# Own places for the first loads, block 0's squares among the sample's tiles, and memory's values for two heads at once

## The chip, the cores and the metric

One core of a Trainium2 chip. The metric is the device time of one execution in microseconds (us), median over runs. The engines work side by side, each on its own instruction queue in order: TensorE (PE; its weight loads are listed as PEld), VectorE (DVE), ScalarE (ACT), GpSimd (POOL), and SyncE (SP), which here only issues DMAs.

## The reference, cut to what matters

A one-layer encoder trunk runs over 1024 prompt tokens and 256 sample tokens, in float32. All projections have 1024 input features.

```python
h = rmsnorm(x, norm_mix_w)
proj = h @ w_in          # DeltaNet q/k/v, decay inputs, gates, spatial-gating halves u and v
...
def spatial_gating_branch(u, v, ln_w, ln_b, w_s, b_s):
    u = jax.nn.gelu(u)
    v = layernorm(jax.nn.gelu(v), ln_w, ln_b)
    ...
def memory_cross_attention(h, mem, w_q, w_kv, w_o):
    q = (h @ w_q).reshape(bsz, seq, XA_HEADS, XA_HEAD_DIM)
    kv = (mem @ w_kv).reshape(bsz, mem.shape[1], 2, XA_HEADS, XA_HEAD_DIM)
    ...
```

The begin of the kernel is the first RMSNorm of the tokens and the product with the columns of w_in for v and the decay inputs (w_sv, 528 columns). "Memory's values" are the second half of kv: 512 normalised memory tokens (256 for each request group) times 1024 x 1024 weights, four heads of 256 columns.

## The kernel before, in words

Activations lie with features on the partitions: eight tiles (k = 0 to 7) of 128 features by n tokens. The tokens form three blocks: block 0 and block 1 (512 prompt tokens each) and block 2, the sample (256 tokens). A product keeps float32 accuracy by three passes: each operand is split into a rounded part hi (ACT copies it to a reduced format) and a rest lo (a subtraction on DVE or POOL), and PE adds hi x hi, lo x hi and hi x lo. `split` (L124 to L126) does that; `split_w` does it for weight tiles, with the rest on POOL until the DeltaNet stage begins, on DVE from there. Weight tiles come in the order of the list `order`; `take` gives the next one and `ahead` splits the one after it. The unsplit weights land in two shared raw buffers.

PE's instructions stay in the order in which the program writes them. The main line of work is written straight on; beside it run side generators, which a planner resumes by its own clock: each matmul adds its columns divided by 2.4 ns, and a side that yields a number of ns is resumed at the first poll (a `yield` of the main line) after that many have passed. So `yield lag` decides how many of the main line's matmuls stand ahead of a side's. Instructions of the other engines are ordered by a list scheduler, by readiness and place in the program.

A norm (class `Norm`) squares each feature tile on ACT (`add`), sums the squares on DVE (L249), lets PE sum over the partitions (a column of ones), takes the inverse root on DVE (L224 to L228, tile nst), lets PE broadcast it, and scales each tile on DVE (`rest`, L284, tile nt). The scaled tile is then split into hi and lo, which are what PE multiplies.

The begin: the sample's x (xs) is loaded, then the first half of w_sv in the two raw buffers, constants, block 0's x (x0) and, when the raw buffers are free again, the second half of w_sv. The sample's norm runs first; block 0's is a side (`other_norms`), whose sum over partitions stands LAG0 = 7500 planner ns behind its begin. `sgv(b)` multiplies a block by both halves of w_sv: for the sample two chunks of 128 tokens by two halves, 24 matmuls of 264 columns each. Then come two gate tiles of the sample (`sgu`), then block 0's `sgv`, which needs block 0's tiles. `ln(cs)` takes the layernorm of v, beginning 1500 planner ns after a block's `sgv`.

Memory's values (`mem_v`): for each head four tiles of 128 memory tokens gather 8 feature tiles in four banks of PSUM, with two weight tiles of 4 features groups x 256 columns; the result is copied by ACT into a staging tile and stored to vd. Meanwhile the sample's DeltaNet scan runs as a side.

Of the kernel before, what the change touches and what calls it, by code (L numbers as in the profile page):

```python
# [17 lines left out]
P = 128  # L18
D = 1024
KT = D // P  # L20
NP, NS = 1024, 256
NTOK = NP + NS
NCH = NTOK // P
NMEM = 256
HEADS = 4
# [16 lines left out]
def f32(ap):  # L42
    return ap.bitcast(F32)
# [11 lines left out]
class Trunk:  # L55
# [44 lines left out]
    def mm(self, out, l, r, start=True, stop=True, more=False):  # L100
        n = 1
        for x in out.shape[1:]:
            n *= x
        if l.dtype == F32R:
            self.clock += max(n, 16) / 2.4 * (1 if n >= 256 else 4)
        else:
            self.clock += (4 * n / 2.4) if n > 1 else 2
        self.nc.tensor.matmul(out, l, r, start=start, stop=stop, skip_group_check=more)  # L108
# [22 lines left out]
    def load(self, i):  # L131
        while self.loaded <= i and self.loaded < len(self.order):
            src = self.order[self.loaded][0]
            raw = self.raw()[:, :1024]
            self.nc.sync.dma_start(raw, src)
            self.raws[self.loaded] = raw
            self.loaded += 1

# [25 lines left out]
def trunk_kernel(ctx: ExitStack, tc: tile.TileContext, a):  # L164
    nc = tc.nc
    V, S, G, T, SY = nc.vector, nc.scalar, nc.gpsimd, nc.tensor, nc.sync
    K = Trunk(ctx, tc, a)
    mm, mm3, tr, split = K.mm, K.mm3, K.tr, K.split
# [7 lines left out]
    wp = K.wp = ctx.enter_context(pool("w", 2))  # L176
    hp = ctx.enter_context(pool("h"))
    pm = ctx.enter_context(pool("pm", 4, space=PSUM))
# [18 lines left out]
        elif job[0] == "gate":  # L197
            order.append((a["w_g"][job[1]], "wp"))
    order += [(a["w_k"][m], "wp") for m in range(KT)]
    order += [(a["w_v"][h, i], "wp") for h in range(HEADS) for i in range(2)]  # L200
    order += [(a["w_ub"][m], "wp") for m in range(KT // 2)]
    order += [(a["w_ua"][m], "wp") for m in range(KT // 2)]
    order += [(a["w_out"][m], "wp" if m < 2 else "wx") for m in range(KT)]
# [13 lines left out]
    def bank(p=pq, tag="b"):  # L217
        return p.tile([P, 512], F32, tag=tag, name="bank")

    def wk(w, k, m=P):  # L220
        return w[0][:, k * m : (k + 1) * m], w[1][:, k * m : (k + 1) * m]
# [66 lines left out]
    def norm(p, xk, n, wcol, sink, pace=1300, step=700, lag=1500):  # L288
        nm = Norm(p, n)
        for k in range(KT):  # L290
            nm.add(xk(k))
            yield step
        yield from nm.rest(xk, wcol, sink, pace, lag=lag)

    def to_h(h, b):
        return lambda k, t: split(h[b][0][:, k, :], h[b][1][:, k, :], t, V if k % 2 else G)
# [37 lines left out]
    def x_load(src, t0, n, name):  # L334
        x = xp.tile([P, KT, 512], F32, tag="x", name=name)[:, :, :n]
        for k in range(0, KT, 2):
            SY.dma_start(x[:, k : k + 2, :], src[:, k : k + 2, t0 : t0 + n])
        return x

    def sv_raw(half):  # L340
        raws = [K.raw() for _ in range(2)]
        for i, raw in enumerate(raws):
            SY.dma_start(raw, a["w_sv"][half][:, i * 1056 : (i + 1) * 1056])
        return raws

    def sv_split(half, raws):
        lo = svp.tile([P, 8 * 264], F32R, tag="lo", name="svl")
        hi = svp.tile([P, 8 * 264], F32R, tag="hi", name="svh")
        for i, raw in enumerate(raws):
            sl = slice(i * 1056, (i + 1) * 1056)  # L350
            split(hi[:, sl], lo[:, sl], raw, V if i else G)
        sv.append((hi, lo))


    xs = hp.tile([P, KT, NS], F32, tag="lo1", name="xs")
    for k in range(0, KT, 2):
        SY.dma_start(xs[:, k : k + 2, :], a["xT"][:, k : k + 2, NP:])
    SY.dma_start(sm, a["small"])
    SY.dma_start(cst[:, C_BD:], a["const"][:, C_BD:])
    sv_raw0 = sv_raw(0)  # L360
    SY.dma_start(cst[:, :C_BD], a["const"][:, :C_BD])
    x_h = act_tiles()

    def first_norm():

        nm = Norm(xp, 512)
        for k in range(0, KT, 2):
            nm.add(xs[:, k : k + 2, :].rearrange("p k t -> p (k t)"))
        nm.n = NS
        yield from nm.rest(lambda k: xs[:, k, :], S_MIX, to_h(x_h, 2), 0, lag=0, halves=2)  # L370

    first = K.side(first_norm())
    sv_split(0, sv_raw0)
    x0 = x_load(a["xT"], 0, 512, "x0")
    sv_split(1, sv_raw(1))
    K.finish(first)

    done = set()

    def other_norms():  # L380
        yield from norm(xp, lambda k: x0[:, k, :], 512, S_MIX, to_h(x_h, 0), 600, 0, LAG0)
        done.add(0)
        x1_ = x_load(a["xT"], 512, 512, "x1")
        yield 3000
        yield from norm(xp, lambda k: x1_[:, k, :], 512, S_MIX, to_h(x_h, 1), 900)
        done.add(1)
        mem = x_load(a["memT"], 0, 512, "mem")
        yield 6000
        yield from norm(xp, lambda k: mem[:, k, :], 512, S_MEM, lambda k, t: SY.dma_start(md[k], t))
# [36 lines left out]
    bias2 = sp.tile([P, 4, P], F32, name="bias2")  # L426
    SY.dma_start(bias2, a["sg_b"].unsqueeze(0).to_broadcast([P, 4, P]))

    def ln(cs):

        yield 1500
        V.tensor_tensor(out=mu[:, cs], in0=s0[:, cs], in1=s1[:, cs], op=ALU.add)
        V.tensor_scalar(out=scr[:, cs], in0=mu[:, cs], scalar1=-1.0 / 512, scalar2=None, op0=ALU.mult)
        V.tensor_scalar(out=mu[:, cs], in0=mu[:, cs], scalar1=1.0 / 512, scalar2=None, op0=ALU.mult)
        for c in range(cs.start, cs.stop):
            junk = sp.tile([P, 512], F32, tag="gt", name="junk", bufs=3)
            S.activation(junk, vg[:, c, :], AF.Square, bias=scr[:, c : c + 1], accum_out=var[:, c : c + 1])
        V.tensor_scalar(out=var[:, cs], in0=var[:, cs], scalar1=1.0 / 512, scalar2=4.0 * EPS, op0=ALU.mult, op1=ALU.add)
        yield 2000
        rsqrt(rs[:, cs], var[:, cs], s0[:, cs])  # L440
        for c in range(cs.start, cs.stop):
            V.tensor_scalar(out=vg[:, c, :], in0=vg[:, c, :], scalar1=mu[:, c : c + 1], scalar2=rs[:, c : c + 1], op0=ALU.subtract, op1=ALU.mult)

    lns = {}
# [52 lines left out]
    def sgv(b):  # L497
        if b < 2:
            K.until(norms, lambda: b in done)
        for half in (0, 1):  # L500
            w = sv[half]
            nv = 264 if half == 0 else 248
            for c in range(4 * b, min(4 * b + 4, NCH)):
                cs = slice((c % 4) * P, (c % 4 + 1) * P)
                hi, lo = x_h[b]
                ps = bank(pm)
                n = 0
                for k in range(KT):
                    wh, wl = wk(w, k, 264)
                    for l, r in ((hi[:, k, cs], wh), (lo[:, k, cs], wh), (hi[:, k, cs], wl)):  # L510
                        mm(ps[:, :264], l, r, n == 0, n == 23)
                        n += 1
                    yield 0
                acc = (s0 if half == 0 else s1)[:, c : c + 1]
                gelu2(sp, ps[:, :nv], vg[:, c, half * 264 : half * 264 + nv], nv, acc)
                if half:
                    V.tensor_copy(ab[:, c, :], ps[:, 248:264])
        lns[b] = K.side(ln(slice(4 * b, min(4 * b + 4, NCH))))
        K.ahead()

    def bias():
# [511 lines left out]
    def staging(n):  # L1033
        staged.append(0)
        return stage[:, len(staged) % 4, :n]
# [28 lines left out]
        S.activation(t, ps, AF.Copy)  # L1064
        S.dma_start(kd[m], t)

    def mem_v(h):
        pss = [bank(pm)[:, :256] for _ in range(4)]
        for i in range(2):
            w = K.take()  # L1070
            for c in range(4):
                cs = slice(c * P, (c + 1) * P)
                for k in range(4):
                    wh, wl = wk(w, k, 256)
                    xh, xl = mhi[:, 4 * i + k, cs], mlo[:, 4 * i + k, cs]
                    for j, (l, r) in enumerate(((xh, wh), (xl, wh), (xh, wl))):
                        mm(pss[c], l, r, i == 0 and k == 0 and j == 0, i == 1 and k == 3 and j == 2)
                    yield 0
                if c == 0:
                    K.ahead()  # L1080
                if i:
                    t = staging(256)
                    S.activation(t, pss[c], AF.Copy)
                    S.dma_start(vd[h, c], t)

    def half_wk(w, i, k):
        return wk(w, 4 * i + k)
# [61 lines left out]
    def rest():  # L1149
        for m in range(1, KT):  # L1150
            yield from mem_k(m)
        for h in range(HEADS):
            yield from mem_v(h)
        yield from up_b()

    ya = None
# [883 lines left out]
A1, A2, A3, A4 = 1200, 800, 2000, 600  # L2040
DEC, CONV = 1200, 600
FIRST_W, PACES, LAGS2 = 9000, (600, 1300, 600), (2800, 9500, 7000)
LAG0, LAGF, LAGF2, PACEF = 7500, (8000, 6000, 1500), (9000, 9000, 2800), 1000

SHARED = ((1, 4, 6), (1, 3, 5, 7), (1, 3, 6))

# [78 lines left out]
```

## Time and profile before

| | |
|---|---|
| runs (us) | 2241.98, 2242.71, 2244.09; median 2242.71 |
| span of the profiled execution | 2242.3 us, 32397 instructions |
| TensorE busy | 2195.8 us (98%) |
| VectorE, ScalarE, GpSimd busy | 1394.7 us (62%), 813.2 us (36%), 531.5 us (24%) |
| mean granted TensorE clock | 0.996 |
| chain that ended last | 82% on TensorE, 7% on VectorE, 5% issue, 3% DMA |

The profiled execution's own time is given as its span, from the first to the last instruction. In a timeline row stand start, duration, engine, line, operation, written tile <- read tiles, shape and number of instructions; in brackets the engine's idle time before it and what ended that. In a row of a stretch stand its length, then for each engine busy time and number of instructions, then PEclk, the granted TensorE clock as a share of full speed, then the DMA engines' share and GB/s.

### The profile page before, as it was taken

To read this page: it belongs to the slowest core of one execution; us is meant where nothing else is said; L and a number is where in the kernel's file an instruction comes from. 1 tells how busy PE (TensorE), PEld (TensorE's weight loads), DVE (VectorE), ACT (ScalarE), POOL (GpSimd) and SP (SyncE) were. 2 spreads that over 40 slices of the span, in tenths; PEclk is the share of its full clock that TensorE was granted. 3 is DMA by queue.
4 is the path that set the end of the run, shared out by engine and by line. 5 is a ranking of instruction groups with operands and counts; after the bars stand their busy time and mean duration, and the time that the engine had idled before them with its cause. 6 is when DMAs were issued, how large, how long until landed. Compare 5 with 4: busy or idle time off the path is not lost.

```text
span 2242.3 us, 32397 instructions
## 1 busy us (share of the span) xinstructions
PE 2195.8 (98%) x12480; PEld 1920.4 (86%) x12480; DVE 1394.7 (62%) x2749; ACT 813.2 (36%) x1473; POOL 531.5 (24%) x355
## 2 busy tenths in 40 slices
PE   6999999999999999999999999999999999999998
PEld 6988888888888899888888888888888888888888
DVE  7767788897985874574634536743444334468575
ACT  5434243333424443222344432433232223243453
POOL 3010000000000000013132332366666666210031
PEclk9999999999999999999999999999999999999999
DMA  5222322223234454973131342232222222393531
GB/s 184 78 81 72 104 72 83 76 65 105 69 108 129 150 141 139 325 231 122 66 109 62 114 169 80 71 111 87 78 89 80 76 78 87 128 367 127 202 109 57
DMA packets 191302, 262.48 MB, mean 117 GB/s; under 512 B 72410, under 2 KB 102698, under 8 KB 191146
## 3 DMA queue, kind: packets, MB, share of 16 engines
q1 hardware_dynamic: 171306, 231.30, 31.6%
q10 hardware_dynamic: 19840, 29.11, 3.6%
q8 instruction: 98, 1.61, 0.3%
q14 instruction: 58, 0.48, 0.1%
HBM read 182.19 MB, written 78.16 MB: 116 GB/s over the span
## 4 chain that ended last, share of the span: by engine, by line
PE 82%; DVE 7%; issue 5%; DMA 3%; ACT 2%; POOL 1%; SPq 0%; ACTq 0%; POOLq 0%; DVEq 0%
PE bank L108 81%; DMA tbd<-stage 1%; PE bank L121 1%; DVE acc L599 1%; DVE wlo L126 1%; DVE nt L284 1%; DVE sw L903 0%; DMA gb<-grd 0%; DVE U L845 0%; DMA yod<-gs 0%; DVE lo L126 0%; DMA stage<-gtd 0%; DVE nacc L249 0%; DVE aT L714 0%; DMA t<-sgd 0%
## 5 line engine op out<-in xcount | busy, mean ns | idle before, releaser
L108 PE MATMUL bank<-hi,whi 128*128 128x512 f32 (+1 forms) x2152 | 766.9, 356 | 0.0
L108 PE MATMUL bank<-lo,whi 128*128 128x512 f32 (+1 forms) x2152 | 752.3, 350 | 0.0
L108 PE MATMUL bank<-hi,wlo 128*128 128x512 f32 (+1 forms) x2152 | 752.1, 349 | 0.0
L108 PEld LDWEIGHTS bank<-hi,wlo 128*128 128x128 f32 x2152 | 407.3, 189 | 53.6
L108 PEld LDWEIGHTS bank<-hi,whi 128*128 128x128 f32 x2152 | 408.3, 190 | 49.4 <-issue 0.2
L108 PEld LDWEIGHTS bank<-lo,whi 128*128 128x128 f32 x2152 | 408.3, 190 | 48.4 <-issue 0.2
L126 POOL TENSOR_TENSOR wlo<-raw,whi 128x1024 fp32r<-128x1024 f32 x72 | 174.8, 2430 | 473.1 <-ACT whi L125 470.1
L125 ACT ACTIVATE whi<-raw 128x1024 fp32r<-128x1024 f32 (+1 forms) x144 | 145.6, 1013 | 279.9 <-PE bank L108 226.5
L108 PE MATMUL bank<-bhl,whi 128*128 128x512 f32 x408 | 126.0, 390 | 0.0
L126 DVE TENSOR_TENSOR wlo<-raw,whi 128x1024 fp32r<-128x1024 f32 (+1 forms) x72 | 82.9, 1153 | 44.0 <-ACT whi L125 41.9
L126 POOL TENSOR_TENSOR wlo<-x,whi 128x1024 fp32r<-128x1024 f32 x40 | 96.5, 2411 | 48.1 <-ACT whi L125 48.1
L1791 DVE TENSOR_TENSOR x<-x,bank 128x512 f32<-128x512 f32 x21 | 14.5, 689 | 126.1 <-ACT x L1586 126.1
L108 PEld LDWEIGHTS bank<-bhl,whi 128*128 128x128 f32 x408 | 76.5, 188 | 16.1 <-ACT whi L125 0.4
L599 DVE SCALAR_TENSOR_TENSOR acc<-craw,sm,acc 128x510 f32<-128x510 f32 (+1 forms) x96 | 73.6, 766 | 20.5 <-ACT acc L597 19.0
L249 DVE TENSOR_TENSOR nacc<-nacc,nsq 128x512 f32<-128x512 f32 (+1 forms) x72 | 59.8, 831 | 35.7 <-ACT nsq L248 34.4
L1599 DVE SCALAR_TENSOR_TENSOR t<-t,x 128x512 f32<-128x512 f32 x42 | 64.0, 1523 | 28.4 <-ACT t L1598 28.4
L108 PE MATMUL bank<-bhl,wlo 128*128 128x512 f32 x204 | 79.6, 390 | 0.5 <-DVE wlo L126 0.5
L745 DVE TENSOR_TENSOR W<-W,UT 128x2 f32<-128x2 f32 (+30 forms) x155 | 73.0, 471 | 10.9 <-DMA W<-in_eye 6.6
L125 ACT ACTIVATE whi<-x 128x1024 fp32r<-128x1024 f32 (+1 forms) x48 | 49.0, 1026 | 79.8 <-PE bank L108 73.6
L962 ACT ACTIVATE gs<-bank 128x512 f32<-128x512 f32 (+1 forms) x60 | 31.2, 520 | 125.2 <-PE bank L108 119.1
L248 ACT ACTIVATE nsq<-x 128x512 f32<-128x512 f32 (+1 forms) x70 | 40.1, 582 | 98.2 <-DVE x L1238 91.2
L1608 DVE SCALAR_TENSOR_TENSOR t<-bank,t 128x512 f32<-128x512 f32 (+1 forms) x44 | 24.5, 558 | 82.3 <-PE bank L108 82.3
(328 smaller groups left out, 4218.6 us busy)
## 6 DMA issues: line engine op xcount, KB each, us to landing
raw<-in_w_gu SPq DMA_DIRECT2D x44, 512.0 KB, 3.4
braw<-gq SPq DMA_DIRECT2D x14, 1024.0 KB, 6.1
raw<-in_w_g SPq DMA_DIRECT2D x20, 512.0 KB, 3.4
gq<-t SPq DMA_DIRECT2D x33, 256.0 KB, 2.0
gtd<-gs ACTq DMA_DIRECT2D x32, 256.0 KB, 2.0
w<-in_w_dn SPq DMA_DIRECT2D x8, 1024.0 KB, 11.5
raw<-in_w_qkv SPq DMA_DIRECT2D x12, 512.0 KB, 3.4
gq<-r SPq DMA_DIRECT2D x22, 256.0 KB, 2.0
```

The lines of the kernel that those rows point to most:

```text
L108: self.nc.tensor.matmul(out, l, r, start=start, stop=stop, skip_group_check=more)
L121: self.nc.tensor.transpose(out, x, ident)
L125: self.nc.scalar.activation(hi, src, AF.Copy)
L126: (eng or self.nc.vector).tensor_tensor(out=lo, in0=src, in1=f32(hi), op=ALU.subtract)
L248: S.activation(sq, x, AF.Square)
L249: (eng or V).tensor_tensor(out=self.acc, in0=self.acc, in1=sq, op=ALU.add)
L284: V.scalar_tensor_tensor(out=t, in0=xk(k), scalar=sm[:, wcol + k : wcol + k + 1], in1=pb[:, :n], op0=ALU.mult, op1=ALU.mult)
L599: V.scalar_tensor_tensor(out=dst, in0=src, scalar=wj, in1=dst, op0=ALU.mult, op1=ALU.add)
L745: V.tensor_tensor(out=t3, in0=u3[:, i:, c:].rearrange("p j c -> p c j"), in1=XL[:, 32 * i + i : 32 * i + 32].unsqueeze(1).to_broadcast([P, ...
L962: S.activation(t, ps, AF.Tanh, scale=0.5)
L1599: V.scalar_tensor_tensor(out=t, in0=t, scalar=1.0, in1=src, op0=ALU.add, op1=ALU.mult)
L1608: V.scalar_tensor_tensor(out=out, in0=u, scalar=sign, in1=t, op0=ALU.mult, op1=ALU.mult)
```

## The change

The begin gets places of its own: `rooms`, two areas that later hold block 1's tiles, take the sample's x, the second half of w_sv, the squares and a second sum. So the second half's loads need not wait for raw buffers; on SP they stand behind x0's. The constants are loaded in two parts, the identity first and the rest last. Block 0's squares are no longer made by its side: while the sample's tiles are split (`first_h`), one square of block 0 goes to ACT ahead of each copy (`issue_after` keeps that order), and the squares are summed in two tiles, on POOL for even k and DVE for odd k; the sum over partitions takes both. LAG0 becomes 4500. The sums of the other norms that use `norm` (block 1, memory) go to POOL. The sample's layernorm begins 9000 planner ns after its `sgv`, not 1500.

Memory's values are made for two heads at once: matmuls of 512 columns in place of 256, weight tiles of 2 feature groups x 2 heads x 256 columns, each loaded with two DMAs of 1 KB pieces, and half as many copies and stores of twice the size.

```diff
@@ class Trunk, load
             raw = self.raw()[:, :1024]
-            self.nc.sync.dma_start(raw, src)
+            for k in range(src.shape[1]) if len(src.shape) == 4 else ():
+                self.nc.sync.dma_start(raw.rearrange("p (k h c) -> p k h c", k=src.shape[1], h=src.shape[2])[:, k], src[:, k])
+            if len(src.shape) != 4:
+                self.nc.sync.dma_start(raw, src)
@@ the order of the weights
-    order += [(a["w_v"][h, i], "wp") for h in range(HEADS) for i in range(2)]
+    for x in range(HEADS // 2):
+        for q in range(4):
+            src = a["w_v"][2 * x : 2 * x + 2, q // 2].rearrange("h p (k c) -> p k h c", c=256)
+            order.append((src[:, 2 * (q % 2) : 2 * (q % 2) + 2], "wp"))
@@ norm
-            nm.add(xk(k))
+            nm.add(xk(k), G)
@@ the begin
-    xs = hp.tile([P, KT, NS], F32, tag="lo1", name="xs")
+    rooms = [hp.tile([P, 4096], F32, tag=tag, name="room") for tag in ("lo1", "hi1")]
+    xs = rooms[0][:, : KT * NS].rearrange("p (k t) -> p k t", t=NS)
+    sv1 = [rooms[1][:, i * 1056 : (i + 1) * 1056] for i in range(2)]
+    squares = [rooms[0][:, 2048 + 512 * i : 2560 + 512 * i] for i in range(4)] + [rooms[1][:, 3072 + 512 * i : 3584 + 512 * i] for i in range(2)]
...
-    SY.dma_start(cst[:, :C_BD], a["const"][:, :C_BD])
+    SY.dma_start(cst[:, :C_TRI], a["const"][:, :C_TRI])
+    x0 = x_load(a["xT"], 0, 512, "x0")
+    for i, raw in enumerate(sv1):
+        SY.dma_start(raw, a["w_sv"][1][:, i * 1056 : (i + 1) * 1056])
+    SY.dma_start(cst[:, C_TRI:C_BD], a["const"][:, C_TRI:C_BD])
...
-    def first_norm():
-
-        nm = Norm(xp, 512)
-        for k in range(0, KT, 2):
-            nm.add(xs[:, k : k + 2, :].rearrange("p k t -> p (k t)"))
-        nm.n = NS
-        yield from nm.rest(lambda k: xs[:, k, :], S_MIX, to_h(x_h, 2), 0, lag=0, halves=2)
-
-    first = K.side(first_norm())
+    norm2, norm0 = Norm(xp, 512), Norm(xp, 512)
+    for k in range(0, KT, 2):
+        norm2.add(xs[:, k : k + 2, :].rearrange("p k t -> p (k t)"))
+    norm2.n = NS
     sv_split(0, sv_raw0)
-    x0 = x_load(a["xT"], 0, 512, "x0")
-    sv_split(1, sv_raw(1))
-    K.finish(first)
+
+    behind = []
+
+    def square(k):
+        if k == 0:
+            dst = norm0.acc
+        elif k == 1:
+            dst = norm0.apart = rooms[1][:, 2560:3072]
+        else:
+            dst = squares[k - 2]
+        behind.append(S.activation(dst, x0[:, k, :], AF.Square).ins)
+        if k > 1:
+            acc = norm0.apart if k % 2 else norm0.acc
+            (V if k % 2 else G).tensor_tensor(out=acc, in0=acc, in1=dst, op=ALU.add)
+
+    def first_h(k, t):
+        if k:
+            square(k - 1)
+        with ExitStack() as st:
+            if behind:
+                st.enter_context(tc.issue_after(behind[-1]))
+            S.activation(x_h[2][0][:, k, :], t, AF.Copy)
+        (V if k % 2 else G).tensor_tensor(out=x_h[2][1][:, k, :], in0=t, in1=f32(x_h[2][0][:, k, :]), op=ALU.subtract)
+
+    K.finish(K.side(norm2.rest(lambda k: xs[:, k, :], S_MIX, first_h, 0, lag=0, halves=2)))
+    square(KT - 1)
+    sv_split(1, sv1)
...
     def other_norms():
-        yield from norm(xp, lambda k: x0[:, k, :], 512, S_MIX, to_h(x_h, 0), 600, 0, LAG0)
+        yield from norm0.rest(lambda k: x0[:, k, :], S_MIX, to_h(x_h, 0), 600, lag=LAG0)
@@ ln, sgv
-    def ln(cs):
-
-        yield 1500
+    def ln(cs, wait):
+
+        yield wait
...
-        lns[b] = K.side(ln(slice(4 * b, min(4 * b + 4, NCH))))
+        lns[b] = K.side(ln(slice(4 * b, min(4 * b + 4, NCH)), 9000 if b == 2 else 1500))
@@ memory's values
-    def mem_v(h):
-        pss = [bank(pm)[:, :256] for _ in range(4)]
-        for i in range(2):
+    def mem_v(hp_):
+
+        pss = [bank(pm) for _ in range(4)]
+        for q in range(4):
             w = K.take()
             for c in range(4):
                 cs = slice(c * P, (c + 1) * P)
-                for k in range(4):
-                    wh, wl = wk(w, k, 256)
-                    xh, xl = mhi[:, 4 * i + k, cs], mlo[:, 4 * i + k, cs]
+                for k in range(2):
+                    wh, wl = wk(w, k, 512)
+                    xh, xl = mhi[:, 2 * q + k, cs], mlo[:, 2 * q + k, cs]
                     for j, (l, r) in enumerate(((xh, wh), (xl, wh), (xh, wl))):
-                        mm(pss[c], l, r, i == 0 and k == 0 and j == 0, i == 1 and k == 3 and j == 2)
+                        mm(pss[c], l, r, q == 0 and k == 0 and j == 0, q == 3 and k == 1 and j == 2)
                     yield 0
                 if c == 0:
                     K.ahead()
-                if i:
-                    t = staging(256)
+                if q == 3:
+                    t = staging(512)
                     S.activation(t, pss[c], AF.Copy)
-                    S.dma_start(vd[h, c], t)
+                    S.dma_start(vd[2 * hp_ : 2 * hp_ + 2, c].rearrange("h p d -> p h d"), t.rearrange("p (h d) -> p h d", h=2))
...
-LAG0, LAGF, LAGF2, PACEF = 7500, (8000, 6000, 1500), (9000, 9000, 2800), 1000
+LAG0, LAGF, LAGF2, PACEF = 4500, (8000, 6000, 1500), (9000, 9000, 2800), 1000
```

More of the change, by code (lines that the diff above doesn't have):

```diff
@@ L1151, in rest @@
             yield from mem_k(m)
-        for h in range(HEADS):
-            yield from mem_v(h)
+        for x in range(HEADS // 2):
+            yield from mem_v(x)
         yield from up_b()
```

## The prediction

> **What bounds the kernel now.** I read the page first, then busy time and granted clock by stretches of the first 60 us, then the timelines of each engine there and where memory's values are made.
>
> ```profile
> span 2242.3 us, 32397 instructions
> PE 2195.8 (98%) x12480; PEld 1920.4 (86%) x12480; DVE 1394.7 (62%) x2749; ACT 813.2 (36%) x1473; POOL 531.5 (24%) x355
> ```
>
> TensorE (PE) is busy 98% of the span and its order is written by hand, so a change pays only where PE idles, runs at a lower clock, or takes less time for the same columns. The diff touches two such places: the begin, and mem_v, around 848 us.
>
> ```profile
> core 0: us, PE busy (x) PEld busy (x) DVE busy (x) ACT busy (x) POOL busy (x), PEclk, DMA share, GB/s
> 24.20:27.63 3.43, 1.38 (x11) 1.17 (x10) 3.33 (x3) 2.57 (x6) 2.94 (x1) 1.00 0.00 0
> 27.63:31.05 3.42, 3.42 (x18) 3.42 (x17) 3.19 (x8) 0.42 (x1) 0.00 (x0) 0.52 0.67 200
> ...
> 44.70:48.10 3.40, 2.01 (x13) 1.38 (x12) 3.40 (x7) 2.57 (x6) 2.07 (x2) 1.00 0.00 0
> 48.10:51.50 3.40, 2.30 (x8) 1.40 (x8) 3.33 (x10) 0.94 (x2) 0.86 (x1) 0.52 0.21 19
> 51.50:54.90 3.40, 3.40 (x17) 3.40 (x17) 2.48 (x10) 1.97 (x4) 0.00 (x0) 0.50 1.01 386
> ```
>
> Each stretch in which PE worked 1.4 to 2.3 us of 3.4 is followed by one at half the granted clock (0.52, 0.50). A gap is paid twice: once idle, and again at half speed.
>
> ```profile
> 15.22 0.59 PE L108 MATMUL bank<-svh,hi 128*128 128x264 f32 x1 [1.02 <-ACT hi L125]
> ...
> 19.81 0.42 PE L108 MATMUL bank<-svl,hi 128*128 128x264 f32 x1
> 20.03 0.42 PE L108 MATMUL bank<-svh,hi 128*128 128x264 f32 x1
> ...
> 27.19 0.39 PE L108 MATMUL bank<-svl,hi 128*128 128x264 f32 x1 [2.05 <-POOL svl L126]
> ...
> 31.49 0.95 PE L108 MATMUL bank<-cst,nacc 128*128 128x1 f32 x8
> 32.30 0.37 PE L108 MATMUL bank<-svh,hi 128*128 128x264 f32 x1
> ...
> 35.29 1.02 PE L108 MATMUL bank<-sw,cst 128*128 128x512 f32 x2
> ...
> 37.49 1.13 PE L108 MATMUL bank<-cst,nst 128*128 128x128 f32 x8 [0.83 <-DVE nst L228]
> ...
> 43.85 0.29 PE L108 MATMUL bank<-svh,hi 128*128 128x264 f32 x1
> ...
> 44.93 0.28 PE L108 MATMUL bank<-svh,hi 128*128 128x264 f32 x1
> ...
> 50.35 0.59 PE L108 MATMUL bank<-svh,hi 128*128 128x264 f32 x1 [0.53 <-ACT hi L125]
> ...
> 55.89 0.28 PE L108 MATMUL bank<-svh,lo 128*128 128x264 f32 x1
> ```
>
> Matmuls of 264 columns start 0.22 us apart on the half clock (19.81, 20.03) and 0.12 on the full one: 43.85 and 44.93 are the first and tenth of block 0. Three losses show. Weight half 1 is late (2.05 us at 27.19, then a half-clock stretch). The broadcast of block 0's norm waits 0.83 us at 37.49. Block 0's tiles trickle in from 44.93 to 51: the matmul at 55.89 is block 0's 47th, and at 0.12 us it could have come 46 x 0.12 = 5.5 us after the first, so a stall-free block 0 could have begun at 50.4. PE was ready at 43.85; 6.5 us are lost. The number to beat is this **equivalent start, 50.4**.
>
> **The begin, step by step.** The rows that price it:
>
> ```profile
> 14.24 1.26 DVE L284 SCALAR_TENSOR_TENSOR nt<-xs,sm,bank 128x256 f32<-128x256 f32 x3
> 15.07 0.61 ACT L245 ACTIVATE nacc<-x 128x512 f32<-128x512 f32 x1
> 19.72 0.42 ACT L125 ACTIVATE hi<-nt 128x256 fp32r<-128x256 f32 x1 [0.24 <-DVE nt L284]
> 16.38 0.73 POOL L126 TENSOR_TENSOR lo<-nt,hi 128x256 fp32r<-128x256 f32 x1 [0.41 <-ACT hi L125]
> 16.41 0.98 DVE L126 TENSOR_TENSOR lo<-nt,hi 128x256 fp32r<-128x256 f32 x1
> 17.82 0.42 DVE L126 TENSOR_TENSOR lo<-nt,hi 128x256 fp32r<-128x256 f32 x1
> 47.62 1.34 POOL L126 TENSOR_TENSOR lo<-nt,hi 128x512 fp32r<-128x512 f32 x1 [0.59 <-ACT hi L125]
> 50.33 0.69 DVE L126 TENSOR_TENSOR lo<-nt,hi 128x512 fp32r<-128x512 f32 x1
> 24.53 1.07 ACT L125 ACTIVATE svh<-raw 128x1056 fp32r<-128x1056 f32 x1
> 24.19 2.95 POOL L126 TENSOR_TENSOR svl<-raw,svh 128x1056 fp32r<-128x1056 f32 x1 [3.91 <-ACT svh L125]
> 38.66 2.07 DVE L284 SCALAR_TENSOR_TENSOR nt<-x,sm,bank 128x512 f32<-128x512 f32 x3 [0.39 <-PE bank L108]
> 33.40 4.71 POOL L126 TENSOR_TENSOR wlo<-raw,whi 128x1024 fp32r<-128x1024 f32 x2 [6.26 <-ACT whi L125]
> ```
>
> *The sample's tiles get slower.* The change adds a wait: each copy to hi stands behind block 0's previous square on ScalarE (ACT). Behind the copy queue the lo subtraction (VectorE, DVE, or GpSimd, POOL) and then PE. ACT now needs 0.61 + 0.42 = 1.03 us a tile, 8.3 us for eight from about 14.7 (the first scaling's 14.24 + 0.42): last copy 22.4, last square 23.0. POOL has four lows and three sums of 512 columns: 4 x 0.73 + 3 x 1.34 = 6.9 (the sum priced by the 512-column low). DVE has eight scalings of 0.42, four lows, three sums of 0.69: 7.1 undisturbed. ACT sets the least, last low at 22.9. The other end is the row at 16.41: that DVE low took 0.98 instead of 0.42 beside POOL's at 16.38. If all two-input operations of the two engines exclude each other, they need 6.9 + 4 x 0.42 + 3 x 0.69 = 10.7 us from the end of the first copy, 15.2: 25.9. I take 24.1, two delays of 0.6 on top of ACT, since scalings and copies fill between.
> The Trainium skill has that rule (SBUF — State Buffer, Who interferes with whom): a DVE instruction with two SBUF inputs and a GpSimd one that reads SBUF take the shared port pair in turns, one fully blocked. This speaks against the change; the trace agrees at 16.41, and by it alone the 25.9 stands.
>
> *Matmuls over the sample.* At three matmuls (0.66 us at half clock) per tile of over 1 us, the clock stays halved. Chunk 0 of half 0 ends at 24.1 + 0.7 = 24.8; of chunk 1's 24 matmuls 13 run at 0.22 up to the next edge of stretches (27.6), 11 at 0.12: 28.9. LAG0 falls from 7500 to 4500, so block 0's sum over partitions stands after matmul 45, not 72 (330 ns of planner's clock for three matmuls). It now sums two tiles: twice 32.30 - 31.49 = 0.81, 1.6 us. Half 0 is done at 30.5.
>
> *Weight half 1.* With places of their own its loads need no freed raw buffers. They are queued behind block 0's on SP; a shorter constant load goes ahead and the rest of the constants behind. ACT comes to it after the last square: 23.0 + 1.07 = 24.1, POOL's low to 27.1 at the price of 24.19. PE wants it at 30.5: the 2.05 us wait and its half-clock stretch go, with 3.4 us of cover. Without the cover, half 1 starts at 27.1, no later than now.
>
> *Up to block 0.* Half 1 is 48 x 0.12 = 5.8; the broadcast 1.1, and I keep its 0.8 us of waiting, since 27 matmuls still stand between sum and broadcast; bias about 0.5; two gate tiles, 48 matmuls of 256 columns, 5.8. 30.5 + 14.0 = 44.5, against 43.85: nothing is gained up to there.
>
> *Block 0's tiles.* The broadcast stands after matmul 72: 30.5 + 24 x 0.12 + 0.8 = 34.2, not 37.49, so the first scaling moves from 38.66 to 35.4. From there to the last low now takes 50.33 + 0.69 - 38.66 = 12.4 us; at that pace it ends at 47.8. PE wants the eighth tile 21 matmuls after 44.5, at 47.0. The sample's layernorm now starts 9000 planner ns after its values, not 1500, and leaves DVE, so the pace should rise. I take 0.4 us of stall: equivalent start 44.9. **The begin gains 50.4 - 44.9 = 5.5 us**; with squares running before the first copy, up to 8.
>
> Sums for the second block and memory go to POOL, seven of 1.34 each; it has no low to make while block 0 is multiplied, and starts those norms earlier. I cost this at nothing; gone, it is 7 x (1.34 - 0.69) = 4.6 us at the second block's start.
>
> **Memory's values.** Each of 384 matmuls of 256 columns becomes half of one of 512.
>
> ```profile
> 773.07 0.40 PE L108 MATMUL bank<-mhi,whi 128*128 128x512 f32 x1
> ...
> 774.90 0.39 PE L108 MATMUL bank<-mhi,wlo 128*128 128x512 f32 x1
> 848.01 0.28 PE L108 MATMUL bank<-whi,mlo 128*128 128x256 f32 x1
> ...
> 849.57 0.28 PE L108 MATMUL bank<-wlo,mhi 128*128 128x256 f32 x1
> raw<-in_w_v SPq DMA_DIRECT2D x4, 512.0 KB, 4.7
> 814.99 0.34 SPq L135 DMA_DIRECT2D raw<-in_w_v  x1
> 828.93 1.06 ACT L125 ACTIVATE whi<-raw 128x1024 fp32r<-128x1024 f32 x1 [0.46 <-DVE UT L815]
> ```
>
> Starts eight apart: 1.83 / 8 = 0.229 us for 512 columns. Thirteen apart: 1.56 / 13 = 0.120 for 256. 384 x 0.120 - 192 x 0.229 = 46.1 - 44.0 = **2.1 us** gained. The page TensorE: Matmul & The Clock Gate of the Trainium skill (Wait — 56ns, not 53.3ns?) gives a warm matmul N/2.4 GHz plus about 2.5 ns; an estimate by it is 192 x 2.5 ns = 0.5 us, where this trace has 2.1.
> Its weights come in two DMAs a tile, in 1 KB pieces. The load issued at 814.99 was copied at 828.93; at a landing of 4.7 us it lay ready 9 us, so even a doubled landing is covered. Evictions, half as many, stay off PE. Side work is polled every 640 planner ns, not 320: a step of the sample's scan can come 0.3 us later; I leave -0.5 to +1 us for it.
>
> **Sum.** 2242.3 - 5.5 - 2.1 = 2234.7; the median of the runs, 2242.71, lies 0.4 above the profiled span, so 2235.1.
>
> **Rivals.** *The shared port bounds the begin* (the skill's rule above, worked from rows): last low at 25.9, chunk 0 ends 26.6, the next stretch is at half clock too, chunk 1 ends about 31.5, half 0 at 33.1, PE reaches block 0 at 47.1, with a stall of 0.7 and part of a half-clock stretch, 48.7. Gain 1.7 + 2.1: 2238.9. For it the 0.98; against it the 0.42 at 17.82, with POOL idle.
> *Memory's values gain nothing*: columns alone set the time, and the 0.229 belongs to another stage. 2242.7 - 5.5 = 2237.2. Against it: both are the same kind of matmul.
> *Slower: POOL becomes the bound.* Raw buffers are free earlier, so the gate weights' lows (4.71 for two) can be placed among the sample's lows and the sums. Last low 25.9 + 4.7 = 30.6, half 0 done at 37.2, block 0 reached at 51.2; if its tiles then trickle as now (6.5), 57.7: 7.3 lost, 2.1 won, 2247.9. With that stall kept, it decides once the last low of the sample comes after about 25.1 (PE then reaches block 0 at 46.0). For it: POOL's slow rows; against: those weights' turn in the program comes after all the sums.
>
> **How the numbers follow.** Forecast 0.60 (2232 to 2238), port 0.20, no gain at memory 0.05, POOL 0.15. A measurement here can tell about 0.2%, 4.5 us, from no change. Faster: 0.60 + 0.05 = 0.65. Same: the port's 0.20 and 0.04 of POOL's, 0.24. Slower: 0.11. The range runs from the forecast with 8 us at the begin and a little more at memory, 2231.5, to inside POOL's case, 2245.
>
> **What would show it.** Right: squares between the copies on ACT; the sample's last low at 23 to 25; no wait on POOL's svl at half 1; block 0 reached near 44 and no half-clock stretch after it; mem_v's matmuls 0.23 us apart. Wrong: a last low beyond 26, a new wait for the norm's sums or for nst, half clock after 48, or mem_v waiting for weights.

## The result, and the profile after

The changed kernel is slower: 2254.55 us, median of 5 runs (2254.43 to 2256.16), against 2242.71 before (5 runs beside them, 2241.57 to 2244.09). The ratio is 1.0055, 95% interval 1.0044 to 1.0066. The forecast was 2235.1 in a range of 2231.5 to 2245.

The page's first lines of the changed kernel:

```profile
span 2252.6 us, 32018 instructions
...
PE 2200.6 (98%) x12296; PEld 1914.7 (85%) x12296; DVE 1393.2 (62%) x2731; ACT 811.0 (36%) x1465; POOL 554.8 (25%) x372
```

TensorE has 184 matmuls less and is busy 4.8 us more. Where that comes from shows in the stretches. The columns are those of the prediction's fence: length, busy time and count of PE, PEld, DVE, ACT and POOL, then the granted clock, the DMA engines' share and GB/s.

```profile
core 0: us, PE busy (x) PEld busy (x) DVE busy (x) ACT busy (x) POOL busy (x), PEclk, DMA share, GB/s
24.20:27.63 3.43, 3.43 (x19) 3.43 (x19) 2.04 (x4) 1.77 (x4) 1.79 (x1) 1.00 0.05 20
27.63:31.05 3.42, 3.42 (x32) 3.42 (x31) 0.61 (x4) 0.39 (x1) 0.00 (x0) 1.00 0.02 5
44.70:48.10 3.40, 2.91 (x22) 2.56 (x22) 3.40 (x7) 1.63 (x5) 1.65 (x1) 1.00 0.54 150
...
51.50:54.90 3.40, 3.40 (x30) 3.40 (x29) 2.16 (x5) 2.74 (x7) 3.17 (x4) 1.00 0.20 71
54.90:58.30 3.40, 1.02 (x9) 0.80 (x7) 3.26 (x5) 1.03 (x2) 3.24 (x3) 0.94 0.00 0
58.30:61.70 3.40, 1.60 (x8) 1.60 (x8) 3.33 (x9) 0.70 (x2) 1.67 (x2) 0.50 0.00 0
...
91.40:94.80 3.40, 1.23 (x7) 0.85 (x7) 3.40 (x4) 0.63 (x1) 3.17 (x3) 1.00 0.03 5
```

Up to 55 us the change does what it was to do: the idle time at 24.20 and the half-clock stretches at 27.63 and 51.50 are gone. (The 1.00 of the first row is not full speed: that row has 19 matmuls where the next, as busy, has 32. They start 0.22 us apart up to 26.98 and 0.12 behind it, as the prediction had it for the stretch up to 27.6.) Then come three holes that the kernel before does not have: at 54.90, at 91.40 and, in memory's values, at 830. In the first two POOL is busy with its sums. The timelines there (start, duration, engine, line, operation, tiles, shape, count, idle time before and its releaser):

```profile
23.26 0.41 DVE L404 TENSOR_TENSOR lo<-nt,hi 128x256 fp32r<-128x256 f32 x1
34.62 2.07 DVE L290 SCALAR_TENSOR_TENSOR nt<-x,sm,bank 128x512 f32<-128x512 f32 x3 [0.39 <-PE bank L108]
43.93 0.29 PE L108 MATMUL bank<-svh,hi 128*128 128x264 f32 x1
...
50.59 9.46 POOL L255 TENSOR_TENSOR nacc<-nacc,nsq 128x512 f32<-128x512 f32 x7 [3.76 <-ACT nsq L254]
58.98 1.08 DVE L233 TENSOR_TENSOR sums<-sums 128x2 f32<-128x2 f32 x1
60.10 0.16 DVE L234 SCALAR_TENSOR_TENSOR sums<-sums 128x2 f32<-128x2 f32 x1
60.10 1.87 PE L108 MATMUL bank<-cst,nacc 128*128 128x1 f32 x8 [4.18 <-POOL nacc L255]
...
85.91 9.73 POOL L255 TENSOR_TENSOR nacc<-nacc,nsq 128x512 f32<-128x512 f32 x7 [6.26 <-ACT nsq L254]
88.84 5.65 DVE L474 TENSOR_SCALAR vg<-vg,sums 128x512 f32<-128x512 f32 x4
91.73 0.49 PE L108 MATMUL bank<-sw,vg 128*128 128x128 f32 x2 [0.58 <-DVE vg L474]
93.14 0.49 PE L108 MATMUL bank<-sw,vg 128*128 128x128 f32 x2 [0.92 <-DVE vg L474]
94.55 0.49 PE L108 MATMUL bank<-sw,vg 128*128 128x128 f32 x2 [0.92 <-DVE vg L474]
```

The same places before:

```profile
62.62 0.69 DVE L249 TENSOR_TENSOR nacc<-nacc,nsq 128x512 f32<-128x512 f32 x1
64.66 0.95 PE L108 MATMUL bank<-cst,nacc 128*128 128x1 f32 x8
88.88 1.91 DVE L442 TENSOR_SCALAR vg<-vg,sums 128x512 f32<-128x512 f32 x4
89.70 1.63 PE L108 MATMUL bank<-sw,vg 128*128 128x128 f32 x8
```

Before, the last sum of the second block ended at 62.62 + 0.69 = 63.31, 1.35 us ahead of TensorE. Now it ends 3.3 us earlier, at 60.05, but TensorE is there 8.7 us earlier, at 60.10 - 4.18 = 55.92, and waits 4.18 us. A VectorE operation on 128x2 numbers takes 0.16 us alone (60.10) and 1.08 beside a GpSimd sum (58.98), and it ends when that sum ends: 50.59 + 9.46 = 60.05. The four multiplications of vg take 5.65 us together beside GpSimd's sums, 1.41 each, and 1.91 without them, 0.48 each. TensorE waits for three of them.

In memory's values (ACT and SP beside PE):

```profile
818.81 0.56 SPq L136 DMA_DIRECT2D raw<-in_w_v  x1
820.39 0.84 SPq L831 DMA_DIRECT2D uc<-usd  x2
...
824.75 11.25 SPq L136 DMA_DIRECT2D raw<-in_w_v  x7
...
829.37 0.39 PE L108 MATMUL bank<-wlo,mhi 128*128 128x512 f32 x1
831.07 1.06 ACT L125 ACTIVATE whi<-raw 128x1024 fp32r<-128x1024 f32 x1
832.18 0.50 PE L108 MATMUL bank<-whi,mhi 128*128 128x512 f32 x1 [2.43 <-ACT whi L125]
...
834.01 0.80 PE L108 MATMUL bank<-wlo,mhi 128*128 128x512 f32 x1 [1.02 <-DVE wlo L126]
```

The tile that PE wants at 830 has its first half loaded at 818.81 and its second only at 824.75: the sample's eight uc loads stand between the two on SP's queue. Its copy comes on ACT at 831.07, behind four staging copies. TensorE waits 2.43 and 1.02 us, and its granted clock is 0.50 from 834.2 to 837.6. Before, no matmul of memory's values waited over 0.2 us.

So much time is there at five places (start of the matmul in us from the span's start, read from the PE timelines; the last two columns are experiments told of below):

| | before | after | two repairs | repairs, sums placed later |
|---|---|---|---|---|
| last hi x hi matmul of block 0's sgv | 75.9 | 77.0 | 74.4 | 72.3 |
| last hi x hi matmul of block 1's sgv | 114.8 | 120.6 | 114.9 | 110.4 |
| first matmul of memory's keys | 742.9 | 746.6 | 743.5 | 738.2 |
| last matmul of up_a | 989.4 | 998.9 | 988.3 | 981.3 |
| span | 2242.3 | 2252.6 | 2241.4 | 2234.4 |

After that place nothing more is won or lost: 1253 us from up_a's end to the end of the span in all four, within 1 us.

### The profile page after: what moved, and what is told of

It is laid out like the page before. It is cut to its first block, busy times and chain, and to the rows that moved or that the text cites. A ratio compares the mean times of both kernels' runs of the same rounds, so it can differ in the third digit from the quotient of the medians.

```text
span 2252.6 us, 32018 instructions
## 1 busy us (share of the span) xinstructions
PE 2200.6 (98%) x12296; PEld 1914.7 (85%) x12296; DVE 1393.2 (62%) x2731; ACT 811.0 (36%) x1465; POOL 554.8 (25%) x372
## 4 chain that ended last, share of the span: by engine, by line
PE 82%; DVE 8%; issue 4%; DMA 3%; ACT 2%; POOL 1%; SPq 0%; ACTq 0%; POOLq 0%; DVEq 0%
PE bank L108 80%; PE bank L121 1%; DVE acc L631 1%; DVE nt L290 1%; DMA braw<-gq 1%; DVE wlo L126 1%; POOL nacc L255 1%; DMA stage<-gtd 0%; DMA tbd<-stage 0%; DVE sw L935 0%; DMA gb<-grd 0%; DVE U L877 0%; DVE lo L126 0%; DVE vg L474 0%; DVE nacc L255 0%
## 5 line engine op out<-in xcount | busy, mean ns | idle before, releaser
L255 POOL TENSOR_TENSOR nacc<-nacc,nsq 128x512 f32<-128x512 f32 x28 | 40.6, 1450 | 174.5 <-ACT nsq L254 172.7
L897 POOL COPY UT<-U 64x512 f32<-64x512 f32 x20 | 13.8, 697 | 251.8 <-PE bank L108 250.2
```

The source lines that it names most:

```text
L255: (eng or V).tensor_tensor(out=self.acc, in0=self.acc, in1=sq, op=ALU.add)
```

## The experiments

Each ran with the kernel before on the same chip, in three groups of four: 5 or 6 runs of e1, e2 and e8, 10 to 12 of each of the others. The table gives medians, that of before in the same group, their difference, and the ratio with its 95% interval; the interval leaves each difference open by about 2 us to either side, by 3 where there are 5 or 6 runs. The profiled executions of e1, e8 and e12 took 3.7 to 5.2 us more than the median of their runs, so their traces may show more waiting than is usual.

| | us | before | difference | ratio |
|---|---|---|---|---|
| e1_dve_sums | 2252.11 | 2242.82 | +9.3 | 1.0039 [1.0025, 1.0053] |
| e2_old_memory | 2249.73 | 2242.82 | +6.9 | 1.0034 [1.0021, 1.0047] |
| e3_begin_only | 2243.81 | 2242.82 | +1.0 | 1.0002 [0.9993, 1.0011] |
| e4_one_load | 2247.94 | 2242.82 | +5.1 | 1.0023 [1.0014, 1.0032] |
| e5_sums_and_load | 2242.21 | 2243.06 | -0.9 | 0.9992 [0.9984, 1.0001] |
| e6_sums_placed_later | 2237.76 | 2243.06 | -5.3 | 0.9975 [0.9967, 0.9984] |
| e7_pool_sums_later | 2247.96 | 2243.06 | +4.9 | 1.0016 [1.0007, 1.0026] |
| e8_before_pool_sums | 2254.30 | 2243.06 | +11.2 | 1.0051 [1.0038, 1.0064] |
| e9_before_wide_values | 2241.38 | 2243.36 | -2.0 | 0.9993 [0.9985, 1.0002] |
| e10_pool_second_block | 2242.52 | 2243.36 | -0.8 | 0.9999 [0.9990, 1.0007] |
| e11_pool_memory | 2242.71 | 2243.36 | -0.7 | 0.9999 [0.9990, 1.0007] |
| e12_lag0_as_before | 2244.45 | 2243.36 | +1.1 | 1.0006 [0.9997, 1.0014] |

### Undoing one part each

The first theory was: the begin's gain was lost to GpSimd's sums, and memory's values to the second load of a tile. Four kernels take parts away.

*e1_dve_sums*, the changed kernel with

```diff
-            nm.add(xk(k), G)
+            nm.add(xk(k))
```

> The changed kernel with one argument less: the sums of squares of the second block and of memory are made on VectorE again, as before; block 0's sums stay on two engines, and memory's values stay as changed. Theory A (the begin is lost to GpSimd's sums): the 4.18 us for which TensorE waited for the second block's sums at 60.1 and the half clock behind it go, so do the waits on vg at 91.7 to 94.6; the last matmul of the second block's gates (120.64 changed, 114.83 before) comes at 109 to 111, and the time is 8 to 11 us under the changed kernel, 2244 to 2247. Theory B (what VectorE no longer gets done comes from the sample's layernorm being started 9000 planner ns later and from the new order of the begin, and GpSimd's sums only show it): VectorE has seven more operations of 0.69 us in the same stretch, so the wait at 60 stays or moves, and the time is within 3 us of the changed kernel, 2252 to 2257.

*e2_old_memory*: the changed kernel with `mem_v`, the order of w_v and its loads as before.

> The changed kernel with memory's values as before: one head at a time, 256 columns, one load per weight tile; the begin as changed. Theory A (the two waits of 2.43 and 1.02 us at 832 to 834 come from the weight tile's second load, queued behind the sample's loads): without the wide tiles no wait of over 0.5 us in memory's values; from the first matmul of memory's keys to the last of up_a 246.5 us as before, not 252.3; time 5 to 6 us under the changed kernel, 2248 to 2250. Theory B (the begin's own delay shifts all side work against the loads, and memory's part is late for that reason): the 252 stays, whichever way the values are made, and without the wide matmuls the time is 0 to 2 us over the changed kernel.

*e3_begin_only*: both edits, so the begin alone.

> The begin of the change alone, without GpSimd's sums for the second block and memory: both of those are made on VectorE, and memory's values are made as before. Theory A (the begin's 5.5 us are really won up to 50 us and only GpSimd's sums and memory's loads lost them): the last matmul of the second block's gates at 109 to 111 where before had 114.8, and the time 4 to 6 us under the kernel before, 2237 to 2239. Theory B (the gain of the begin is given back anyway, at the second block's norms or by the order of the DeltaNet stage behind it): time within 2 us of before, 2241 to 2245.

*e4_one_load*: the changed kernel with w_v laid out by tiles on the host, and

```diff
-            src = a["w_v"][2 * x : 2 * x + 2, q // 2].rearrange("h p (k c) -> p k h c", c=256)
-            order.append((src[:, 2 * (q % 2) : 2 * (q % 2) + 2], "wp"))
+            order.append((a["w_v"][x, q], "wp"))
```

> The changed kernel with each of the eight weight tiles of memory's values loaded by one transfer instead of two; the host lays the tile out in the order in which it is used. The matmuls of 512 columns, GpSimd's sums and all else stay. Theory A (the second transfer of a tile goes out 6 us after the first because the sample's loads stand between them on SyncE's queue): the waits of 2.43 us at 832 and 1.02 us at 834 go, with the half clock behind them, and the time is 4 to 6 us under the changed kernel, 2248 to 2251. Theory B (the copy to whi is late on ScalarE because the staging copies of the finished group and the side work polled half as often stand ahead of it): the waits stay within 1 us of their sum, and the time is within 1.5 us of the changed kernel, 2253 to 2256.

Memory's part came out as theory A had it. With one load (e4) the tile's copy starts at 824.20, 6.9 us earlier than in the changed kernel and ahead of the staging copies, and the two waits are gone:

```profile
818.46 0.56 SPq L135 DMA_DIRECT2D raw<-in_w_v  x1
...
824.20 1.06 ACT L125 ACTIVATE whi<-raw 128x1024 fp32r<-128x1024 f32 x1 [5.34 <-PE bank L108]
```

That is 11.8 - 5.1 = 6.7 us, against 11.8 - 6.9 = 4.9 for giving up the wide matmuls altogether (e2). The 1.8 between them fits the matmuls' own gain of 2.1, but lies within the noise of the two.

The begin's part did not. With VectorE's sums (e1) the vg rows are back at 1.91 us for four, but block 1's last hi x hi matmul comes at 114.7, not at 109 to 111, and the median fell by 2.5 us instead of 8 to 11, to the low end of theory B's range; its runs spread from 2249.19 to 2255.79. The begin alone (e3) gains nothing: theory B. In its PE timeline TensorE still waits, now 1.17 us, for the second block's sums:

```profile
58.31 1.05 PE L108 MATMUL bank<-cst,nacc 128*128 128x1 f32 x8 [1.17 <-DVE nacc L249]
```

The last of them ended at 58.25, 5.1 us earlier than before. But TensorE came 7.5 us earlier, at 57.1: its own gain of 5, and a new place in the order. Counted in the trace, 293 of TensorE's matmuls stand ahead of the second block's sums over partitions before and 272 after; ahead of memory's 529 and 502. LAG0 had been cut by 3000 planner ns, and every later sum of that side moved up with it: 21 x 0.12 = 2.5 us. The margin of 1.35 became a wait at the second block, with a half-clock stretch behind it. At memory the margin of 2.5 became waits of 0.72 us for the sums and 1.53 for nst, with the clock at 1.00 behind them. This is theory P of the next runs: place in the order. A rival was not tested alone: the sample's layernorm, which the change starts later, now has part of its work on VectorE and ScalarE in this same stretch and may make the sums late.

### Both repairs, and the place

*e5_sums_and_load* joins e1 and e4.

> The changed kernel with both repairs at once: the sums of the second block and of memory on VectorE, and one load for each weight tile of memory's values. If the two losses simply add: the lost time of memory's values falls by 6 to 8 us as with the one load alone, the second block's part by 3, and the time is 2241 to 2244, about that of the kernel before, with the wait of 1.2 to 1.4 us for the second block's sums still there. If the one hides the other (an earlier TensorE meets the loads of memory's weights later): 2246 or more.

*e6_sums_placed_later* adds to it

```diff
-    def norm(p, xk, n, wcol, sink, pace=1300, step=700, lag=1500):
+    def norm(p, xk, n, wcol, sink, pace=1300, step=700, lag=4500):
```

> The kernel of the two repairs with one number more: the sums over partitions of the second block and of memory are placed 3000 planner ns later in TensorE's order (lag 4500 in place of 1500), which is what LAG0 took away in front of them. Theory P (place in the order): with VectorE's sums TensorE now comes to them 7.5 us earlier than before, 5 by its own gain and 2.5 because they stand at its matmul 272 in place of 293, while the sums are ready only 5 us earlier; so placed 25 matmuls later there is no wait for nacc at 57 and none at 92, no half clock behind them, and the begin's 5 us stay: 2235 to 2239, faster than before. Theory Q (the chain of the second block's norm is late by itself, through its load, and whatever follows it waits): the wait moves to nst or to the second block's first tile, and the time stays at that of the two repairs, 2241 to 2244.

*e7_pool_sums_later*: the same lag, with GpSimd's sums (e4 and the line of e6).

> The changed kernel with one load for each weight tile of memory's values and the sums placed 3000 planner ns later, but with GpSimd's sums kept. If GpSimd's sums cost by themselves and not only by being waited for: the wait for nacc at 60 shrinks from 4.2 to about 1.5 us, but VectorE's multiplications of vg beside GpSimd's seven sums still take 1.4 in place of 0.5 us and TensorE waits for them near 90 as before; 2243 to 2247, at least 4 us over the same kernel with VectorE's sums. If only the place in TensorE's order matters: within 2 us of that kernel.

*e12_lag0_as_before*: e5 with

```diff
-LAG0, LAGF, LAGF2, PACEF = 4500, (8000, 6000, 1500), (9000, 9000, 2800), 1000
+LAG0, LAGF, LAGF2, PACEF = 7500, (8000, 6000, 1500), (9000, 9000, 2800), 1000
```

> The kernel of the two repairs with LAG0 back at 7500, which puts block 0's sum over partitions 27 matmuls later in TensorE's order and the later sums with it, back to where they stood before. Theory P (place): no wait for the second block's sums, but block 0's first scaling comes at about 39 in place of 35, its tiles trickle behind TensorE again and the begin's gain falls from 5 to about 2 us: 2239 to 2243. If block 0's earlier broadcast is worth nothing: 2235 to 2238, as with the later placed sums.

e5 came out at the time of before, as expected, with the wait still there. e6 is faster than both kernels: one number took 4.5 us more off. Its timeline has no wait for nacc and a short one for nst, and the vg rows are quick:

```profile
60.07 0.95 PE L108 MATMUL bank<-cst,nacc 128*128 128x1 f32 x8
64.77 1.16 PE L108 MATMUL bank<-cst,nst 128*128 128x128 f32 x8 [0.58 <-DVE nst L230]
...
84.99 1.91 DVE L470 TENSOR_SCALAR vg<-vg,sums 128x512 f32<-128x512 f32 x4
...
86.08 1.36 PE L108 MATMUL bank<-sw,vg 128*128 128x128 f32 x8
```

The stretch behind e5's wait, at 0.69 of the clock there (first row), runs at full clock in e6 (second):

```profile
58.30:61.70 3.40, 3.40 (x22) 3.40 (x23) 2.06 (x14) 0.82 (x2) 0.00 (x0) 0.69 0.00 0
```

```profile
58.30:61.70 3.40, 3.40 (x32) 3.40 (x31) 3.19 (x17) 0.60 (x2) 0.00 (x0) 1.00 0.00 0
```

So theory P's forecast came out, in time and in trace: to place the sums later is enough. With GpSimd's sums the later place brought nothing that can be measured (e7, +4.9 against e4's +5.1). The wait for the second block's sums shrinks from 4.18 to 0.99 us, but one of 1.68 for nst comes behind it, and the vg waits stay. Undoing LAG0 instead (e12) takes the wait for the sums away too, but the scaling of block 0's tiles then starts at 39.85 and TensorE waits for them:

```profile
39.85 2.06 DVE L286 SCALAR_TENSOR_TENSOR nt<-x,sm,bank 128x512 f32<-128x512 f32 x3
...
47.68 0.39 PE L108 MATMUL bank<-svh,hi 128*128 128x264 f32 x1 [1.15 <-ACT hi L125]
...
50.91 0.59 PE L108 MATMUL bank<-svh,lo 128*128 128x264 f32 x1 [1.24 <-DVE lo L126]
```

It came out 1.1 us over before, above the 2239 to 2243 expected, and 6.4 over e6. The earlier sum of block 0 is needed; what must not move with it are the later ones.

### One part alone

*e8_before_pool_sums*: the kernel before with `nm.add(xk(k), G)`.

> The kernel before with nothing but GpSimd's sums for the second block and for memory. In it the second block's last sum is ready 1.35 us ahead of TensorE and its squares come slower than one a 1.34 us, so no wait for nacc at 64.7. If GpSimd blocks VectorE: the four multiplications of vg at 88.9, 0.5 us each, fall among memory's sums and take 1.2 to 1.4 us each, TensorE waits 2 to 3 us for them and runs a stretch at half clock, 2245 to 2248. If the sums cost only where they are waited for: 2242 to 2244.

*e10_pool_second_block* and *e11_pool_memory*: e6 with GpSimd's sums in one of the two norms, whose call gets `eng=G`; without it the sums are VectorE's.

```diff
-            nm.add(xk(k))
+            nm.add(xk(k), eng)
```

> The kernel of the two repairs and the later placed sums, with GpSimd's sums again for the second block alone. If the wait in order is the cost: GpSimd's last sum ends at about 60, TensorE comes to it at 59.5 to 60, so a wait of 0.5 to 1.2 us for nacc, 1 to 2 us for nst, and a half-clock stretch, 3 to 5 us over that kernel, 2240 to 2243. If the loss of the ten microseconds lies at memory's norm: within 2 us of it.

> The same kernel with GpSimd's sums for memory alone. If GpSimd's sums block VectorE's multiplications of vg: those four take 1.4 in place of 0.5 us, three waits of 0.6 to 1.1 us on TensorE near 88 to 93 and a half-clock stretch behind them, 5 to 7 us over the kernel of the two repairs and the later placed sums, 2243 to 2245. If the ten microseconds lie at the second block's norm: within 2 us of it.

*e9_before_wide_values*: the kernel before with the `mem_v` of the change and one load for each tile.

> The kernel before with memory's values alone changed: two heads at once in matmuls of 512 columns, and each weight tile loaded by one transfer. The begin is that of before. The forecast's step of 2.1 us (384 starts of 0.120 against 192 of 0.229): 2240.5 to 2241.5. If the polling of side work at half the rate or the loads cost something even with one transfer a tile: 2242 to 2245, with a wait of over 1 us in memory's values.

e8 missed: 11.2 us lost where 2 to 5 were expected. The edit was wider than I took it for: in the kernel before, `norm` serves block 0 too, so five of its sums stand on POOL ahead of the second weight half, and TensorE waits 5.30 us for it instead of 2.05. The rest is as expected: no wait for the second block's sums, and the four vg at memory's sums.

```profile
20.99 6.72 POOL L249 TENSOR_TENSOR nacc<-nacc,nsq 128x512 f32<-128x512 f32 x5 [0.74 <-ACT nsq L248]
27.66 3.44 POOL L126 TENSOR_TENSOR svl<-raw,svh 128x1056 fp32r<-128x1056 f32 x1
31.15 0.59 PE L108 MATMUL bank<-svl,hi 128*128 128x264 f32 x1 [5.30 <-POOL svl L126]
...
93.97 5.63 DVE L442 TENSOR_SCALAR vg<-vg,sums 128x512 f32<-128x512 f32 x4
```

e10 and e11 split the price of the sums in the kernel e6: each takes back 4.5 to 4.7 us of its 5.3, give or take 2 to 3, together 9.1, and both at once (e7) cost 10.2. Where the sums stand early in TensorE's order the same step is worth 2.5 us (e1 against the changed kernel) or 6.0 (e5 against e4), since VectorE's sums are then waited for too. At the second block it is the wait itself, and that for nst behind it, 0.58 us in e6 (e10):

```profile
60.45 1.05 PE L108 MATMUL bank<-cst,nacc 128*128 128x1 f32 x8 [0.98 <-POOL nacc L251]
67.91 1.16 PE L108 MATMUL bank<-cst,nst 128*128 128x128 f32 x8 [1.64 <-DVE nst L230]
```

At memory no one waits for the sums; the price is VectorE's vg beside them (e11):

```profile
85.69 5.62 DVE L470 TENSOR_SCALAR vg<-vg,sums 128x512 f32<-128x512 f32 x4
...
88.56 0.49 PE L108 MATMUL bank<-sw,vg 128*128 128x128 f32 x2 [0.92 <-DVE vg L470]
```

e9 gave -2.0 us beside the -2.1 forecast; its interval reaches just past no change.

## Why the prediction was wrong

**The begin up to block 0: right.** Last low forecast at 24.1, measured 23.26 + 0.41 = 23.67; no wait for weight half 1; block 0 reached at 43.93 (44.5 forecast), its first scaling at 34.62 (35.4), one stall of 0.49 us (0.4), no half clock behind it. Block 0's 47th matmul, at 55.89 before, starts at 50.44: the begin's 5.5 us were won, 5.45. The reason holds only in part. ScalarE was to set the pace of the sample's tiles, but waited 0.98 and 1.10 us for scalings, while VectorE worked without a pause from 15.19 to 23.67 and its sums of 512 columns took 1.21 to 1.36 us beside GpSimd's work where 0.69 was counted. That is the mechanism of the rival of the shared port, at a smaller price than its 25.9; that the last low still fell near the forecast was in part luck.

**"Sums for the second block and memory go to POOL ... I cost this at nothing": the step that failed.** Two things were wrong in it. The cover was counted as if TensorE kept its time: "starts those norms earlier" is true, by 4.2 us (first sum at 50.59, before at 54.76), but TensorE came 8.7 us earlier, and the 1.35 us by which the sums had been ready before was not read from the trace at all. And the sum of 4.6 us priced only the longer sums at the second block's start; it left out what they hold up. The contention that the prediction weighed for the sample's tiles was not weighed for these fourteen sums, though four large VectorE operations run beside the last seven. Measured: 4.5 us at the second block (e10 against e6), 4.7 at memory (e11), each give or take 2 to 3.

This is the rule of the Trainium skill (SBUF — State Buffer, Who interferes with whom) that a VectorE instruction which needs the port pair shared with GpSimd is held until the other's instruction ends. The trace agrees, down to operations on 128x2 numbers (0.16 to 1.08 us). That GpSimd's sums slow vg is shown by e11 (5.62 us for four, 1.91 in e6); that the port is the way is the page's account, which no run here tests apart.

**"LAG0 falls from 7500 to 4500": half worked.** The prediction placed block 0's own sum by it and stopped. The same generator places the sums of the second block and of memory, so they moved up 21 and 27 matmuls. That cost 4.5 us even with VectorE's sums (e5 against e6).

**"Its weights ... lay ready 9 us, so even a doubled landing is covered": wrong term.** The landing was not doubled; a transfer of a split tile took 3.8 us, median. What was doubled is the number of places in SP's queue, and the second one lay 5.9 us behind the first. The prediction counted the DMAs and not what stands between them. Price 6.7 us.

**"2.1 us gained" by the wide matmuls: right**, 0.23 us apart as in the stage that served as measure, and -2.0 with e9, though its interval reaches from -3.4 to +0.4. The polling at half the rate showed no cost that can be told from noise. The estimate of 0.5 us from the figure of the Trainium skill (TensorE: Matmul & The Clock Gate, Wait — 56ns, not 53.3ns?) is not borne out by the starts, 0.120 and 0.23 us apart; the medians alone do not exclude it.

**The rivals.** The one rival that ended slower put POOL's bound among the sample's lows, with a chance of 0.15. POOL was at fault, but 30 us later. The section on what would show it wrong named three signs, a new wait for the norm's sums, half clock after 48, and mem_v waiting for weights, and all three came; each deserved a price instead of a mention.

With the three faults mended the forecast's sum of 7.6 us is there in one profile (2242.3 - 2234.4 = 7.9), of a run 1.6 us under e6's median, and to two thirds in the medians (5.3). In the chain of medians: +11.8, one load +5.1, VectorE's sums -0.9, later place -5.3.

## What to carry to other kernels

When a change makes the bounding engine arrive earlier at one place, read from the trace how far ahead of it every later operand was ready: margins smaller than the gain become waits, and a delay constant shared by a chain moves the whole chain. Work put on an idle engine is priced by whose instructions it holds up, not by its own engine's idle time. A transfer split in two needs two places in its queue; look at what stands between them.

## What was not expected of the hardware

The same work got another granted clock in another execution. In the kernel before and in e5 TensorE waits 1.31 us for vg, at 130.34 and 130.44, and is as busy around it (2.08 and 2.09 us of 3.40). Behind it the kernel before keeps the full clock, and e5 runs at half of it, for two stretches; the row of before first, then e5's:

```profile
131.20:134.60 3.40, 3.32 (x20) 2.78 (x20) 3.03 (x7) 1.02 (x2) 0.00 (x0) 1.00 0.39 151
```

```profile
131.20:134.60 3.40, 3.40 (x16) 2.95 (x15) 3.03 (x7) 0.63 (x1) 0.00 (x0) 0.51 0.43 155
```

So a gap is not always paid twice, which is what the prediction read from the stretches of the begin. Nor does the clock come back after the same time. The kernels e2 and e4 have the same instructions up to memory's values, and in both TensorE is busy without a gap from 24.10 to 30.90; e2's rows first, then e4's:

```profile
24.10:27.50 3.40, 3.40 (x16) 3.40 (x17) 1.75 (x3) 1.77 (x4) 2.11 (x1) 0.50 0.03 13
27.50:30.90 3.40, 3.40 (x18) 3.40 (x18) 0.28 (x2) 0.00 (x0) 0.00 (x0) 0.50 0.00 0
```

```profile
24.10:27.50 3.40, 3.40 (x20) 3.40 (x20) 1.92 (x3) 1.77 (x4) 1.93 (x1) 0.62 0.09 39
27.50:30.90 3.40, 3.40 (x32) 3.40 (x31) 0.78 (x6) 0.39 (x1) 0.00 (x0) 1.00 0.02 5
```

e2 stays at half clock until 36.97, where its matmuls change from 0.22 us apart to 0.12, and reaches block 0 at 48.2 instead of 43.7. The Trainium skill (TensorE: Matmul & The Clock Gate, What's actually happening) says that the window over which the clock gate looks is free-running, so that the same kernel differs from run to run, which agrees. It says too that about 3.4 us of sustained work bring the full clock. In e4 2.9 us of it did (23.77 to about 26.7), in e2 5.2 us did not (23.93 to 29.16); then came sixteen matmuls of one column, the sums over partitions, and 4.5 us of products until the clock rose (32.43 to 36.97). Whether matmuls of one column count as work, and where a window begins, no run here shows. Both cases may be part of the spread between runs of one kernel (e4's lie between 2244.80 and 2254.56), and are a reason to read single profiles of the begin beside the medians.
